# An encoder trunk of six stages on one core: x loaded from another queue, the mLSTM's divide behind its own mix, attention's sink exponentials behind the next copy of values, the last block's h ahead of a split

## The chip, the cores and the metric

The kernel runs on one core of a Trainium2 chip. A core has TensorE (PE, matrix products), VectorE (DVE), ScalarE (ACT), GpSimd (POOL) and SyncE (SP, which here only starts transfers), and 16 DMA engines that all queues share. The metric is the time of one execution on the device in microseconds (us); lower is better. The kernel before took 940.04 us, the median of three runs (939.75, 940.04, 940.04).

## The reference

The input x has 256 rows (tokens) of 1024 float32 values. Two layers follow one another, each of three steps, and every step ends in a layer norm of a scaled x plus the step's result:

```python
def swiglu(x, w_in, w_out):
    gu = x @ w_in
    g, u = gu[..., :D_FF], gu[..., D_FF:]
    return (jax.nn.silu(g) * u) @ w_out

for l in range(DEPTH):      # DEPTH = 2, D_FF = 2816
    x = layer_norm(ALPHA * x + 0.5 * swiglu(x, ffn_w_in[l, 0], ffn_w_out[l, 0]), ln_g[l, 0], ln_b[l, 0])
    y = mlstm_mixer(x, ...) if l == 0 else window_attention(x, ...)
    x = layer_norm(ALPHA * x + y, ln_g[l, 1], ln_b[l, 1])
    x = layer_norm(ALPHA * x + 0.5 * swiglu(x, ffn_w_in[l, 1], ffn_w_out[l, 1]), ln_g[l, 2], ln_b[l, 2])
```

The mLSTM mixer (layer 0) has four heads. For each head and direction the weighted scores are multiplied with the values and divided by a denominator, the two directions are added, each head is normalised and multiplied by the sigmoid of an output gate:

```python
num = einsum('bhcjs,bhcsv->bhcjv', s_qk, v) + s_inter[..., None] * einsum('bhcvd,bhcjd->bhcjv', C0, q)
den = jnp.maximum(jnp.abs(den), jnp.exp(-m_out))
h = num / den[..., None]
...
h = (h - mu) * lax.rsqrt(var + LN_EPS)
out = jax.nn.sigmoid(o) * h * norm_g
return out @ w_out
```

The attention (layer 1) has 16 query heads of 64 on four key heads, a window of 128 tokens, a distance bias, and for each head a sink: a logit that takes part in the maximum and in the sum of the softmax but has no value:

```python
m = jnp.maximum(jnp.max(s, axis=-1, keepdims=True), sink_l)
pe = jnp.exp(s - m)
attn = pe / (jnp.sum(pe, axis=-1, keepdims=True) + jnp.exp(sink_l - m))
```

## The kernel before

**Products.** Every float32 product is made of three matmuls on operands that are split in two parts: high by high, high by low, low by high. A piece of weights of 128 partitions by 1024 columns (512 KB) lands as `w_raw` or `s_raw`; ACT copies its high part (`w_hi`), DVE subtracts it from the raw piece (`w_lo`). There are ten buffers for split pieces (`RING`), four for `w_raw` and six for `s_raw`. The class `Weights` (L142 to L312) orders loads and splits; `W.done` (L294) frees used pieces and lets further ones be split. x is kept transposed as `xT_hi` and `xT_lo`: PE transposes it in pieces of 128 by 128, ACT copies the high part, DVE makes the rest. Most compute instructions are issued by one helper, so their line in the profile is L133; tiles tell them apart.

**Six stages.** FFN of layer 0 (block 0), mLSTM, FFN (block 2), FFN of layer 1 (block 3), attention, FFN (block 5). The instruction order on each engine is the order of the program. `Paced` (L49) keeps estimated times of PE, DVE, ACT and the loads, and in the FFN stages it is asked after each matmul whether a split or a sum of weights should be put in at this place; outside the FFN stages the places and numbers of splits stand in constants.

**Loads.** SP issues nearly all loads, x's four quarters among them: a quarter of x, a weight, a quarter, a weight, two quarters, then weights (L436 to L442). POOL issues the loads that add to what is in memory (L262: in each FFN group two pieces of `s_raw`) and, right at the start, seven small loads (L453 to L462): the norm's gain `gcol`, the gates' weights `gw`, the gates' four biases and the sinks.

**FFN block.** A first part of the hidden columns is computed plainly (`b_mm`, with `b_silu` on ACT and `b_mul` on DVE, whose result is `hh`). Then come three groups, in each a plain part and `seven` (L720): a form of the product that needs seven instead of eight products of half the size, on sums of x (`S1` to `S4`, made by `x_one`, `x_two`, `x_rest`) and sums of weights. Its intermediate results are called g, e and u; `tr` transposes such a piece for the second product, and its copies are called `h_hi` and `h_lo`. At a block's end `tail` computes the rest of the second product and the layer norm, whose two halves of x (x0 and x1, 128 tokens each) are transposed for the next stage; the transposes of x1 are handed over as `pending` and run inside the next stage, behind as many pieces as `PEND` says. In block 0, PE begins with 10 transposes of an identity matrix, four transposes of x, 10 more of the identity, and four more of x (L585 to L590); the results of the transposes of the identity are used nowhere.

**mLSTM.** In turns of one head: a piece of the output gate's product, `scores(h)`, `mix(h-1)` (PE makes numerators and denominators in four banks `py`; ACT takes the absolute denominators), `divide(h-2)` ahead of `scores(h)`, and `combine` and `settle` (mean and variance by DVE, the power −0.5 by POOL at L1005, which gives `hrs`, and the normalising by DVE). `divide` is a maximum and a reciprocal on `den` by DVE, two copies scaled by 1/den from PE's banks by ACT, and two multiply-adds by DVE. With the copies PE's banks come free.

**Attention.** Eleven steps (L1290). In step st, PE makes the values of head pair st−3, the transposes (`turn`) of pair st−2 in two halves, and the scores of pair st; ACT makes the four exps of the scores and two exps of the sink (`es`); POOL adds them, takes the power −1 and scales the scores in four instructions (`scale`, L1228 to L1232), which the next step's `turn` transposes. Between these lies filling work: `q_rest`, the rest of the projection of q (copied out to `q_hi` and `q_lo`), cut in steps by `QC`, and from step 4 on parts of the output projection; `FB` says how many pieces of it come ahead of the turn, `PU` how many splits of weights go in. `values` ends in a copy `q_hi` by ACT and a remainder `q_lo` by DVE.

Of the kernel before, what the change touches and what calls it, by code (L numbers as in the profile page):

```python
# [11 lines left out]
AF = mybir.ActivationFunctionType  # L12
# [16 lines left out]
PU = [2, 1, 2, 1, 1, 1, 1, 1, 0, 1, 1, 2]  # L29
QC = [4, 16, 21, 27, 32]  # L30
SW = 1
FB = [1, 0, 2, 3, 0, 0, 0, 0, 1, 1, 0]
CT = [0, 1]
LC = [1, 0, 0, 0, 0, 1]
TD = [0, 3, 2, 0, 2, 2]
MP = [1, 0, 0, 0, 1, 0, 1, 1, 0, 0, 0, 0, 2, 2, 2]
PD = [8, 0, 5, 9, 6]
PEND = [6, 4, 6, 6, 6]
# [10 lines left out]
class Paced:  # L49
# [266 lines left out]
def trunk_kernel(ctx: ExitStack, tc: tile.TileContext, x, ffn_w_in, ffn_w_out, ln_g, ln_b, ml_w_in, ml_gate_b,  # L316
# [136 lines left out]
    nc.gpsimd.dma_start(gcol, ml_norm_g[0].rearrange("(c p) -> p c", p=128))  # L453
    gw = consts.tile([128, 8, 16], F32, name="gw")
    nc.gpsimd.dma_start(gw, ml_w_in[0, :, 3072:3088].rearrange("(k p) g -> p k g", p=128))
    gbias = consts.tile([128, 1], F32, name="gbias")
    nc.gpsimd.memset(gbias, 0.0)
    for g in range(4):
        r = 64 * (g % 2) + 32 * (g // 2)
        nc.gpsimd.dma_start(gbias[r:r + 4], ml_gate_b[0, 4 * g:4 * g + 4].rearrange("(p o) -> p o", o=1))  # L460
    sink = consts.tile([128, 16], F32, name="sink")
    nc.gpsimd.dma_start(sink, bass.AP(tensor=at_sink.tensor, offset=at_sink.offset, ap=[[0, 128], [1, 16]]))  # L462
    neg_sink = consts.tile([128, 16], F32, name="neg_sink")
    nc.gpsimd.tensor_scalar(neg_sink, sink, -1.0, None, op0=OP.mult)
    neg_id = consts.tile([128, 128], FR, name="neg_id")
    nc.vector.tensor_scalar(neg_id, ident, -1.0, None, op0=OP.mult)
# [104 lines left out]
    def ffn(l, i, n, pending, last):  # L571
        with ExitStack() as ph:
# [11 lines left out]
            if start:  # L584
                warm(10)  # L585
                to_xT(0, xt[0], ybank, (0,))
                W.split(1)
                warm(10)
                to_xT(1, xt[1], ybank, (0,))
                W.split(2)  # L590
# [79 lines left out]
            else:  # L670
                W.open(pool, ends[bound[0]])
                for t in range(2):
                    ps = [wbank(), wbank()]
                    for m in range(2):
                        for a in range(4):
# [5 lines left out]
                            if t == 1 and a % 2:  # L681
                                [[None, lambda: x_raw(0), None, lambda: x_raw(1)], [None, x_one, None, x_two]][m][a]()
# [4 lines left out]
                    b_mul(sg, ps[1])  # L687
                W.done()
# [31 lines left out]
            def seven(full, unit_turn):  # L720
# [54 lines left out]
            for g in range(GROUPS):  # L775
# [34 lines left out]
                turn = seven(g < GROUPS - 1, unit_turn)  # L810
            nc.filler = None
# [7 lines left out]
    def mlstm(l, n, pending, last):  # L819
        with ExitStack() as ph:  # L820
# [227 lines left out]
            divide(2)  # L1048
# [35 lines left out]
    def attn(l, n, pending, last):  # L1084
        with ExitStack() as ph:
# [106 lines left out]
            def scores(j, between):  # L1192
# [24 lines left out]
                for t in range(2):  # L1217
# [4 lines left out]
                for a in range(2):  # L1222
                    nc.scalar.activation(es[:, :, a], nm[:, :, a], AF.Exp, bias=sink[:, 2 * j + a:2 * j + a + 1])
                stat[j] = sm, es
# [65 lines left out]
            for st in range(11):  # L1290
# [8 lines left out]
                if 0 <= st - 1 < 8:  # L1299
                    scale(st - 1)  # L1300
# [14 lines left out]
                if st < 8:  # L1315
                    scores(st, late)
# [53 lines left out]
```

## Time and profile before

| what | us |
|---|---|
| median of three runs | 940.04 |
| the profiled execution | 940.39 |
| its span, first to last instruction | 938.7 |
| PE busy | 923.0 (98%) |
| DVE busy | 795.3 (85%) |
| ACT busy | 542.9 (58%) |
| POOL busy | 103.0 (11%) |

The profile is of one execution. A row of a timeline has the start in us, the duration in us, the engine, the line, the operation, the tile written and those read, the sizes, the count, and in brackets the idle time of the engine just ahead with what ended it. A row of waits has the engine, the tile it was about to write, what it waited for, and then the total in us, the number of waits and the longest. A row of windows has the stretch in us, its length, busy time and count for PE, PEld (the load of weights into PE), DVE, ACT and POOL, then PE's granted clock as a share of the full one, the busy share of the DMA engines and the GB/s moved. Matmuls are pipelined, and busy times on PE overlap: starts tell more than durations.

### The profile page before, as it was taken

To read this page: it belongs to the slowest core of one execution; us is meant where nothing else is said; L and a number is where in the kernel's file an instruction comes from. 1 tells how busy PE (TensorE), PEld (TensorE's weight loads), DVE (VectorE), ACT (ScalarE), POOL (GpSimd) and SP (SyncE) were. 2 spreads that over 40 slices of the span, in tenths; PEclk is the share of its full clock that TensorE was granted. 3 is DMA by queue.
4 is the path that set the end of the run, shared out by engine and by line. 5 is a ranking of instruction groups with operands and counts; after the bars stand their busy time and mean duration, and the time that the engine had idled before them with its cause. 6 is when DMAs were issued, how large, how long until landed. Compare 5 with 4: busy or idle time off the path is not lost.

```text
span 938.7 us, 12456 instructions
## 1 busy us (share of the span) xinstructions
PE 923.0 (98%) x4464; PEld 768.6 (82%) x4464; DVE 795.3 (85%) x967; ACT 542.9 (58%) x765; POOL 103.0 (11%) x181
## 2 busy tenths in 40 slices
PE   8999999999999999999999999999999999999996
PEld 7888888889978788888888888887888888888885
DVE  5899997796687889988888898978877798898975
ACT  5666756347563547575635576563567554757460
POOL 2010101011110000101010101010445300000100
PEclk9999999999999999999999999999999999999998
DMA  8969773646534949695559597736533376869531
GB/s 261 367 167 331 211 258 70 221 135 197 186 97 147 316 160 314 175 340 135 163 156 347 116 329 211 270 71 221 162 132 112 90 230 241 237 212 314 159 88 45
DMA packets 98461, 187.54 MB, mean 200 GB/s; under 512 B 6720, under 2 KB 37456, under 8 KB 98400
## 3 DMA queue, kind: packets, MB, share of 16 engines
q1 hardware_dynamic: 91648, 174.09, 54.2%
q0 software_dynamic: 6752, 12.66, 8.5%
q8 instruction: 35, 0.57, 0.3%
q14 instruction: 26, 0.21, 0.1%
HBM read 185.68 MB, written 1.05 MB: 199 GB/s over the span
## 4 chain that ended last, share of the span: by engine, by line
PE 76%; DVE 11%; ACT 4%; DMA 4%; issue 3%; POOL 1%; SPq 0%; DVEq 0%; ACTq 0%; POOLq 0%
PE pw L133 47%; PE py L133 28%; DVE w_lo L133 5%; DMA w_raw<-in_ffn_w_in_dram 2%; ACT w_hi L133 2%; DMA w_raw<-in_ffn_w_out_dram 1%; DVE s_raw L133 1%; DMA s_raw<-in_ffn_w_in_dram 1%; ACT sc L133 1%; DVE x L133 1%; DVE h L133 1%; ACT S_hi L133 0%; DVE S L133 0%; DVE e L133 0%; DVE sc L133 0%
## 5 line engine op out<-in xcount | busy, mean ns | idle before, releaser
L133 DVE TENSOR_TENSOR w_lo<-w_raw,w_hi 128x1024 fp32r<-128x1024 f32 (+1 forms) x237 | 280.9, 1216 | 19.7 <-ACT w_hi L133 17.7
L133 ACT CAST w_hi<-w_raw 128x1024 fp32r<-128x1024 f32 (+1 forms) x237 | 241.1, 1048 | 78.3 <-DMA w_raw<-in_ffn_w_out_dram 22.6
L133 PE MATMUL pw<-w_hi,xT_hi 128*128 128x512 f32 x560 | 222.4, 397 | 0.2 <-ACT xT_hi L133 0.2
L133 PE MATMUL pw<-w_hi,xT_lo 128*128 128x512 f32 x560 | 218.7, 391 | 0.0
L133 PE MATMUL pw<-w_lo,xT_hi 128*128 128x512 f32 x560 | 218.3, 390 | 0.1
L133 ACT CAST w_hi<-s_raw 128x1024 fp32r<-128x1024 f32 x144 | 148.4, 1052 | 93.8 <-DVE s_raw L133 57.8
L133 DVE TENSOR_TENSOR w_lo<-s_raw,w_hi 128x1024 fp32r<-128x1024 f32 x144 | 172.6, 1219 | 21.4 <-ACT w_hi L133 21.3
L133 PE MATMUL py<-w_hi,h_hi 128*128 128x512 f32 x352 | 138.2, 393 | 0.3 <-ACT h_hi L133 0.3
L133 PE MATMUL py<-w_hi,h_lo 128*128 128x512 f32 x352 | 137.3, 390 | 0.2 <-DVE h_lo L133 0.2
L133 PE MATMUL py<-w_lo,h_hi 128*128 128x512 f32 x352 | 137.2, 390 | 0.2 <-DVE w_lo L133 0.2
L133 PEld LDWEIGHTS pw<-w_hi,xT_lo 128*128 128x128 f32 x560 | 105.1, 188 | 23.1 <-DVE xT_lo L133 0.8
L133 PEld LDWEIGHTS pw<-w_lo,xT_hi 128*128 128x128 f32 x560 | 105.3, 188 | 21.2 <-DVE w_lo L133 0.7
L133 PEld LDWEIGHTS pw<-w_hi,xT_hi 128*128 128x128 f32 x560 | 105.2, 188 | 20.6 <-ACT xT_hi L133 0.6
L133 DVE TENSOR_TENSOR s_raw<-s_raw 128x1024 f32<-128x1024 f32 x72 | 87.0, 1219 | 0.7
L262 POOL DMA_DIRECT2D s_raw<-in_ffn_w_in_dram x24 | 29.0, 1209 | 497.1 <-DVE w_lo L133 379.0
L133 PEld LDWEIGHTS py<-w_hi,h_lo 128*128 128x128 f32 x352 | 66.0, 188 | 15.1 <-DVE h_lo L133 1.4
L133 PEld LDWEIGHTS py<-w_lo,h_hi 128*128 128x128 f32 x352 | 66.1, 188 | 13.9 <-DVE w_lo L133 0.6
L133 PEld LDWEIGHTS py<-w_hi,h_hi 128*128 128x128 f32 x352 | 66.1, 188 | 13.9 <-ACT h_hi L133 0.7
L133 PE MATMUL pw<-w_hi,S_hi 128*128 128x512 f32 x192 | 74.9, 390 | 0.0
L133 PE MATMUL pw<-w_hi,S_lo 128*128 128x512 f32 x192 | 74.7, 389 | 0.0
L133 PE MATMUL pw<-w_lo,S_hi 128*128 128x512 f32 x192 | 74.7, 389 | 0.0
L133 DVE TENSOR_TENSOR h_lo<-pw,h_hi 128x512 fp32r<-128x512 f32 x44 | 30.2, 687 | 23.7 <-ACT h_hi L133 23.3
(215 smaller groups left out, 1110.0 us busy)
## 6 DMA issues: line engine op xcount, KB each, us to landing
w_raw<-in_ffn_w_out_dram SPq DMA_DIRECT2D x88, 512.0 KB, 5.3
s_raw<-in_ffn_w_in_dram SPq DMA_DIRECT2D x72, 512.0 KB, 6.1
w_raw<-in_ffn_w_in_dram SPq DMA_DIRECT2D x56, 512.0 KB, 5.3
w_raw<-in_ffn_w_in_dram SPq DMA_DIRECT2D x96, 256.0 KB, 4.5
s_raw<-in_ffn_w_in_dram POOLq DMA_DIRECT2D x24, 512.0 KB, 5.9
w_raw<-in_ml_w_in_dram SPq DMA_DIRECT2D x24, 512.0 KB, 4.6
w_raw<-in_at_w_in_dram SPq DMA_DIRECT2D x12, 512.0 KB, 4.3
w_raw<-in_ml_w_out_dram SPq DMA_DIRECT2D x8, 512.0 KB, 3.7
```

The costliest lines, as they stand in the source:

```text
L133: r = f(out, *args, **kw)
L262: nc.gpsimd.dma_start(t.rearrange("p (k f) -> p k f", k=self.words[w]["k"]), v, accum_op=OP.add)
```

## The change

- The four loads of x are issued on ACT's queue, at its very beginning, and no longer by SP; SP's queue begins with the weights.
- The seven small loads of POOL, with the clearing of the biases' tile, the negated sinks (POOL) and the negated identity `neg_id` (DVE), go into a function that is called in block 0 when its first group has been issued. They come behind the first two accumulating loads on POOL's queue.
- The transposes of the identity at the start are 14 and 8 instead of 10 and 10.
- mLSTM: `divide(h)` follows `mix(h)` at once, ahead of `settle(h-1)`; before, it came one turn later, ahead of the next scores. In the order of PE nothing moves by this.
- Attention: a pair's two sink exps, and the exps of the scores of as many halves as `EX` leaves (2 − EX[j]), go into a function `rest` that runs in the next step, behind the copy `q_hi` of values and ahead of `scale`. The first unit list `QC` gives one piece more of q's projection ahead of the first step; `FB` and `PU` are new.
- FFN blocks behind the first: `x_two` comes behind `b_mul` of the second half. In the last group of each, the transposes of u0 (and so the copy `h_hi`) come ahead of the splits of `W.done`.
- `PEND[1]` is 2 instead of 4: in block 2 the transposes of x1 come six matmuls earlier. The other changes in `PEND`, `PD` and `TD` change the number of splits at places outside the FFN blocks.

```diff
-PU = [2, 1, 2, 1, 1, 1, 1, 1, 0, 1, 1, 2]
-QC = [4, 16, 21, 27, 32]
+PU = [2, 0, 1, 2, 1, 2, 1, 1, 0, 1, 1, 4]
+QC = [5, 13, 21, 27, 32]
-FB = [1, 0, 2, 3, 0, 0, 0, 0, 1, 1, 0]
+FB = [1, 0, 1, 3, 2, 1, 0, 0, 1, 1, 0]
+EX = [0, 1, 2, 2, 2, 2, 1, 2]
-TD = [0, 3, 2, 0, 2, 2]
+TD = [0, 3, 2, 0, 2, 1]
-PD = [8, 0, 5, 9, 6]
-PEND = [6, 4, 6, 6, 6]
+PD = [8, 0, 7, 8, 5]
+PEND = [6, 2, 6, 6, 6]
...
-    def load(self, ap, source):
-        if isinstance(source, list):
+    def load(self, ap, source, engine=None):
+        if engine is not None:
+            engine.dma_start(ap, source)
+        elif isinstance(source, list):
...
-        nc.load(xt[t][:, s_], x[0, t * 128:(t + 1) * 128, s_])
+        nc.load(xt[t][:, s_], x[0, t * 128:(t + 1) * 128, s_], nc.nc.scalar)
...
+    def small_loads():
+        nc.gpsimd.dma_start(gcol, ml_norm_g[0].rearrange("(c p) -> p c", p=128))
+        nc.gpsimd.dma_start(gw, ml_w_in[0, :, 3072:3088].rearrange("(k p) g -> p k g", p=128))
+        nc.gpsimd.memset(gbias, 0.0)
+        for g in range(4):
+            r = 64 * (g % 2) + 32 * (g // 2)
+            nc.gpsimd.dma_start(gbias[r:r + 4], ml_gate_b[0, 4 * g:4 * g + 4].rearrange("(p o) -> p o", o=1))
+        nc.gpsimd.dma_start(sink, bass.AP(tensor=at_sink.tensor, offset=at_sink.offset, ap=[[0, 128], [1, 16]]))
+        nc.gpsimd.tensor_scalar(neg_sink, sink, -1.0, None, op0=OP.mult)
+        nc.vector.tensor_scalar(neg_id, ident, -1.0, None, op0=OP.mult)
...
-                warm(10)
+                warm(14)
                 to_xT(0, xt[0], ybank, (0,))
                 W.split(1)
-                warm(10)
+                warm(8)
...
-                                [[None, lambda: x_raw(0), None, lambda: x_raw(1)], [None, x_one, None, x_two]][m][a]()
+                                [[None, lambda: x_raw(0), None, lambda: x_raw(1)], [None, x_one, None, lambda: None]][m][a]()
...
                     b_mul(sg, ps[1])
+                x_two()
                 W.done()
...
-                product(qa, of(4, 1), False, end4)
+                product(qa, of(4, 1), False, end4 if full else lambda: (end4(), tr(hB, 0, v["u0"])))
                 if full:
                     down(1)
-                else:
-                    tr(hB, 0, v["u0"])
...
                 turn = seven(g < GROUPS - 1, unit_turn)
+                if start and g == 0:
+                    small_loads()
...
                 if h > 1:
-                    divide(h - 2)
                     spare()
                 scores(h, (lambda: combine(h - 2)) if h > 1 else None)
                 if h:
                     mix(h - 1)
+                    divide(h - 1)
...
-            divide(2)
             combine(2)
...
+                def exps(t):
                     s_ = sc[j, t]
                     for a in range(2):
                         nc.scalar.activation(s_[:, a], s_[:, a], AF.Exp, bias=nm[:, t, a:a + 1],
                                              scale=slope[2 * j + a], accum_out=sm[:, t, a:a + 1])
+
+                def rest():
+                    for t in range(EX[j], 2):
+                        exps(t)
+                    for a in range(2):
+                        nc.scalar.activation(es[:, :, a], nm[:, :, a], AF.Exp, bias=sink[:, 2 * j + a:2 * j + a + 1])
+                    stat[j] = sm, es
+
+                for t in range(EX[j]):
+                    exps(t)
+                return rest
...
                 if 0 <= st - 1 < 8:
+                    rest()
                     scale(st - 1)
...
-                    scores(st, late)
+                    rest = scores(st, late)
```

More of the change, by code (lines that the diff above doesn't have):

```diff
@@ L452, in trunk_kernel @@
     gcol = consts.tile([128, 8], F32, name="gcol")
-    nc.gpsimd.dma_start(gcol, ml_norm_g[0].rearrange("(c p) -> p c", p=128))
     gw = consts.tile([128, 8, 16], F32, name="gw")
-    nc.gpsimd.dma_start(gw, ml_w_in[0, :, 3072:3088].rearrange("(k p) g -> p k g", p=128))
     gbias = consts.tile([128, 1], F32, name="gbias")
[L457 to L460, printed above, removed]
     sink = consts.tile([128, 16], F32, name="sink")
-    nc.gpsimd.dma_start(sink, bass.AP(tensor=at_sink.tensor, offset=at_sink.offset, ap=[[0, 128], [1, 16]]))
     neg_sink = consts.tile([128, 16], F32, name="neg_sink")
-    nc.gpsimd.tensor_scalar(neg_sink, sink, -1.0, None, op0=OP.mult)
     neg_id = consts.tile([128, 128], FR, name="neg_id")
-    nc.vector.tensor_scalar(neg_id, ident, -1.0, None, op0=OP.mult)
+    def small_loads():
[8 more added lines that the diff above has]
+        nc.vector.tensor_scalar(neg_id, ident, -1.0, None, op0=OP.mult)
     def mm3(o, l, r, start, stop, onto=False):
@@ L1216, in scores @@
                     between()
-                for t in range(2):
+                def exps(t):
                     s_ = sc[j, t]
@@ L1221, in scores @@
                                              scale=slope[2 * j + a], accum_out=sm[:, t, a:a + 1])
-                for a in range(2):
-                    nc.scalar.activation(es[:, :, a], nm[:, :, a], AF.Exp, bias=sink[:, 2 * j + a:2 * j + a + 1])
-                stat[j] = sm, es
+                def rest():
[7 more added lines that the diff above has]
+                return rest
             def scale(j):
```

## The prediction

> **What bounds the kernel now.** I read the page first (busy shares, then the chain that ended last):
>
> ```profile
> span 938.7 us, 12456 instructions
> ...
> PE 923.0 (98%) x4464; PEld 768.6 (82%) x4464; DVE 795.3 (85%) x967; ACT 542.9 (58%) x765; POOL 103.0 (11%) x181
> ...
> PE 76%; DVE 11%; ACT 4%; DMA 4%; issue 3%; POOL 1%; SPq 0%; DVEq 0%; ACTq 0%; POOLq 0%
> ```
>
> TensorE (PE) is busy 98% and carries 76% of the chain. The change leaves the products alone, so it can only shorten the times in which PE waits. Second view, the list of PE's waits (total us, count, longest):
>
> ```profile
> PE py L133 <- DMA x<-in_x_dram: 1.5, 1, 1.5
> PE py L133 <- DVE ident L133: 1.5, 1, 1.5
> PE py L133 <- ACT h L133: 1.3, 2, 0.8
> PE pw L133 <- DVE q_lo L133: 1.0, 2, 0.8
> PE py L133 <- DVE w_lo L133: 0.4, 2, 0.2
> PE pw L133 <- DVE e L133: 0.4, 1, 0.4
> PE pw L133 <- DVE pr_lo L133: 0.3, 1, 0.3
> PE py L133 <- ACT h_hi L133: 0.3, 1, 0.3
> PE pw L133 <- DVE kp_lo L133: 0.3, 1, 0.3
> PE pw L133 <- ACT kp_hi L133: 0.2, 1, 0.2
> PE py L133 <- DVE h_lo L133: 0.2, 1, 0.2
> PE pw L133 <- ACT xT_hi L133: 0.2, 1, 0.2
> PE pw L133 <- DVE hh L133: 0.2, 1, 0.2
> ```
>
> The list holds 7.8 us in all, under 1% of the span: that is nearly all there is to win. What a wait really costs is read from the starts of the matmuls around one of them, in PE's timeline:
>
> ```profile
> 63.16 0.39 PE L133 MATMUL pw<-w_hi,S_lo 128*128 128x512 f32 x1
> 63.39 0.39 PE L133 MATMUL py<-w_hi,h_hi 128*128 128x512 f32 x1
> 63.97 0.50 PE L133 MATMUL py<-w_lo,h_hi 128*128 128x512 f32 x1 [0.20 <-DVE w_lo L133]
> 64.31 0.39 PE L133 MATMUL py<-w_hi,h_lo 128*128 128x512 f32 x1
> ```
>
> Undisturbed starts lie 0.23 apart; 63.39 to 64.31 is 0.92 for two, 0.46 too long, though the idle shown is 0.20. So a wait costs its idle plus about 0.25: the overlap of matmuls is lost too. I use that below.
>
> **Start: x by ScalarE's queue, the small loads off POOL, 14 + 8 warm-up transposes for 10 + 10.**
>
> ```profile
> 1.45 2.40 PE L133 MATMUL py<-ident 128*128 128x128 f32 x10 [1.45 <-DVE ident L133]
> ...
> 9.42 0.39 PE L133 MATMUL pw<-w_hi,xT_lo 128*128 128x512 f32 x1
> 11.27 1.26 PE L133 MATMUL py<-ident,x 128*128 128x128 f32 x8 [1.47 <-DMA x<-in_x_dram]
> 12.29 0.47 PE L133 MATMUL pw<-w_hi,xT_hi 128*128 128x512 f32 x1
> 12.77 0.50 PE L133 MATMUL pw<-w_lo,xT_hi 128*128 128x512 f32 x1
> ```
> ```profile
> 0.00:5.40 5.40, 3.95 (x18) 3.56 (x19) 0.46 (x2) 1.69 (x2) 4.10 (x12) 1.00 0.60 188
> 5.40:12.70 7.30, 5.75 (x33) 4.29 (x32) 3.79 (x6) 3.65 (x7) 2.24 (x4) 1.00 1.00 328
> ```
>
> PE finishes the first weight at 9.65 (9.42 plus one distance), then stands until x's second half has landed, at 11.27. In the windows the last two columns are the DMA engines' busy share and GB/s: 1.00 and 328 after 5.4 us, so bytes set the pace, and the order of requests decides who waits. SP's queue now sends two halves of x and two weights alternately, and x's second half third. On ACT's queue all of x leaves beside the first weights. x and two weights are 2 MB: 188 GB/s to 5.4 us gives 1.0 MB, the other 1.0 at 328 takes 3.2, so all of it is there at about 8.7 us, against 11.27 for x now. The price: x's first half shares the engines with the first weight and lands later than now, when its transposes follow the first ten at once at 3.85 (1.45 + 2.40); sharing alike with the first weight, I take 0.8 more, 4.65. The four more transposes cover it (0.24 each, so 14 end at 4.8), and the two extra in total cost under 0.5. The first weight's product so ends about 0.6 later, at 10.25; x's eight transposes follow without a wait (now 1.02, from 11.27 to 12.29, part of it the restart; I take 0.85), end 11.1, and the second weight's cast and remainder are early enough:
>
> ```profile
> 10.41 1.05 ACT L133 CAST w_hi<-w_raw 128x1024 fp32r<-128x1024 f32 x1 [2.74 <-DMA w_raw<-in_ffn_w_in_dram]
> ```
> ```profile
> 11.49 1.22 DVE L133 TENSOR_TENSOR w_lo<-w_raw,w_hi 128x1024 fp32r<-128x1024 f32 x1 [3.10 <-ACT w_hi L133]
> ```
>
> The cast waits for the landing at 10.4 and DVE for the cast, until 12.71; with all landed at 8.7 the pair ends near 11.2. So 12.29 becomes 11.1 (1.2), and the 0.25 to 0.5 lost at 12.77 goes too: 1.5. I give 0.3 back for the third weight's remainder, which then comes due sooner. **−1.2**; from −2.1 (the whole wait, 1.47 + 0.25, and the one at 12.77) to +0.3 (x no earlier, first product later).
>
> POOL's small loads also leave the first 14 us:
>
> ```profile
> q0 software_dynamic: 224, 0.08, 7.0%
> ...
> gcol<-in_ml_norm_g_dram POOLq DMA_DIRECT2D x1, 4.0 KB, 6.9
> ```
>
> 7.0% of 14 us is 1.0 us of every engine, and supports the −1.2; I count nothing more for it. The trace speaks against the gain, too: at a share of 1.00 another issuer adds no bytes, which is rival 1. The Trainium skill ("DMA: Bandwidth & Descriptors", section "Issuing engines are not separate DMA queues") says the same as a rule: transfers started by several engines interleave on the same 16 DMA engines, and issuing from several saves only the sequencer's time. The share of 1.00 agrees with the first half; whether the order in which requests arrive is worth something beside it, no run here has shown.
>
> **Small loads in their new place.** They are queued behind POOL's two accumulating loads of block 0, so at about 63.2:
>
> ```profile
> 61.96 1.21 POOL L262 DMA_DIRECT2D s_raw<-in_ffn_w_in_dram  x1 [2.24 <-DVE w_lo L133]
> ```
>
> Queued behind them on POOL are only the next group's accumulating loads; their first readers are in the mLSTM. DVE's negated identity (0.23) joins them at about 81 us. I count **0**: between 66 and 180 us the list of PE's waits is empty. The upper bound is a rival.
>
> **mLSTM: the divide behind its own mix.** In DVE's order the two settling instructions (now waiting for POOL) come behind the divide, which now starts at 257.6 behind them:
>
> ```profile
> 256.90 0.74 DVE L133 TENSOR_SCALAR h<-h,hmv,hrs 128x256 f32<-128x256 f32 x2 [0.60 <-POOL hrs L1005]
> ```
>
> The divide starts about 1.3 earlier (0.60 of waiting, 0.74 of work), so ACT's copies of h release PE's banks earlier and both waits for h go (1.3 idle, two restarts: 1.8). But DVE's work stays the same; only its 0.60 waits go, about 0.9 in two rounds once what refills them is taken off, and a later wait for w_lo (281.67, 0.2 idle) comes due sooner. So I keep half: **−0.9**, between −1.8 and −0.3.
>
> **Block 2 (second FFN): transposes of x six matmuls earlier.**
>
> ```profile
> 306.96 1.28 DVE L133 SCALAR_TENSOR_TENSOR x<-x,rs,ln_b 128x1024 f32<-128x1024 f32 x1
> 308.56 1.03 PE L133 MATMUL py<-ident,x 128*128 128x128 f32 x8
> ```
>
> Six distances are 1.4, so PE would arrive at 307.2 while x ends at 308.24: a new wait of 1.1. It frees the 0.2 (0.45) for xT_hi later, and the 0.4 (0.65) for e, since DVE works ahead where it stood. 1.1 − 0.45 − 0.65 = 0; for DVE's work kept busy I take **−0.2**, from −0.5 to +0.8 (only part comes back).
>
> **Ends of the FFN blocks.** h's copy ahead of a split: the one wait for h_hi (0.3) goes, but h_lo on DVE stays behind its e, so **−0.2** (−0.4 to 0). S2 behind the product hh: the 0.2 for hh goes, **−0.35** (−0.45 to 0). The other constants move no instruction.
>
> **Attention.** At the turn of one head's second half:
>
> ```profile
> 709.51 0.47 ACT L133 ACTIVATE es<-nm,sink 128x2 f32<-128x2 f32 x2
> ...
> 710.24 0.35 ACT L133 CAST q_hi<-pw 128x256 fp32r<-128x256 f32 x1
> ...
> 710.77 0.41 DVE L133 TENSOR_TENSOR q_lo<-pw,q_hi 128x256 fp32r<-128x256 f32 x1
> ...
> 711.24 0.66 PE L133 MATMUL pw<-ident,sc 128*128 128x128 f32 x4 [0.84 <-DVE q_lo L133]
> 711.46 1.85 POOL L1232 TENSOR_SCALAR sc<-sc,sm 128x256 f32<-128x256 f32 x4
> ```
>
> q_hi stands behind the sink exps es; with these in the next step, q_lo comes 0.4 sooner, and the work dealt ahead of the turn covers the rest. The list shows five waits in this stage: 1.8 idle, 3.0 with restarts. The one at 711.24 goes (1.1), those at the start shrink with the added q matmuls (0.6), one more of 0.3 to 0.5 goes: 2.1. Given back: 0.6, where two splits now come ahead of q_lo on DVE in one step. **−1.5**; from −2.2 to +0.7. The sink exps themselves (0.47 for two) stay on ACT, which is 58% busy; who waits for them is POOL's scaling (1.85 for four), read by the next turn.
>
> **Sum.** −1.2 − 0.9 − 0.2 − 0.2 − 0.35 − 1.5 = −4.35. The profiled execution took 940.39, its span 938.7 and 1.7 outside, and stands 0.35 above the median of 940.04. 940.39 − 4.35 = **936.0**.
>
> **The rivals.** (1) x comes no earlier: engines at 1.00 carry the same bytes, and only issues are saved. For it: that share; against: x's second half is third in the queue now. Without the −1.2 it is 937.3 (rounded up). (2) The sink exps make POOL late: they now follow another copy on ACT, POOL's chain for a head starts after them, and turns wait for POOL instead of q_lo. Against: the chain for a head has until the next step. −1.5 becomes +0.7: 938.2. Both together: 939.5. (3) Slower: the small loads at 63.2 hold the weight stream. For it: alone at the start gcol took 6.9 from issue to landing for 4 KB and the row at 63.97 shows the lead of w_lo there at nothing, so a hold of 6.9 could reach PE whole: 936.0 + 6.9 = 942.9. It decides from a hold of 4.4 on. Against it: by the 7.0% above all the small loads together took 1.0 of each engine, a seventh of that hold, and between 66 and 180 PE waits for nothing; a hold of 1.0 would give 937.0.
>
> **How the numbers follow.** Forecast 0.61, (1) 0.14, (2) 0.10, both 0.07, (3) 0.08. The forecast's own range is 934.0 to 938.2: about half of the terms' bounds, since they won't all fall on one side. To hold 8 in 10 it goes from 933.8 to 939.6, which takes in (1), (2) and both. A measurement tells 0.2% (1.9 us) from no change: faster is below 938.2, slower above 941.9. Faster: nearly all of the forecast, most of (1), half of (2): 0.75. Slower: (3) and mishaps not listed: 0.10. Same: 0.15.
>
> **What would show it.** Right: no wait for x, second weight near 11 us; no waits for h; in attention none above 0.5 for q_lo; a new wait of about 1 us at 307. Wrong: x's transposes still wait past 11; waits for w_lo between 64 and 80; turns waiting for POOL's sc.

## The result and the profile after

The changed kernel takes 935.21 us (median of 5 runs, 934.8 to 936.01) against 940.04 for the kernel before (5 runs, 938.35 to 940.48). The ratio is 0.9953 with a 95% interval of 0.994 to 0.9966: 0.5% faster. The forecast was 936.0 with a range of 933.8 to 939.6. The profiled execution took 935.12.

Its page has these lines (busy shares, then the chain that ended last); the span is 933.4:

```profile
PE 920.0 (99%) x4466; PEld 769.0 (82%) x4466; DVE 795.5 (85%) x967; ACT 541.4 (58%) x765; POOL 101.5 (11%) x181
...
PE 83%; DVE 9%; DMA 2%; ACT 2%; issue 2%; SPq 1%; POOL 0%; DVEq 0%; ACTq 0%; POOLq 0%
```

No engine has much less to do (PE is busy 920.0 us for 923.0). PE carries 83% of the chain for 76% before, which fits that fewer of its waits are left. The list of PE's waits in the changed kernel (total us, count, longest; the helper's line is now L136):

```profile
PE py L136 <- DVE ident L136: 1.5, 1, 1.5
PE py L136 <- DVE x L136: 0.9, 1, 0.9
PE pw L136 <- ACT e L136: 0.9, 1, 0.9
PE py L136 <- DMA x<-in_x_dram: 0.7, 2, 0.4
PE pw L136 <- DVE h L136: 0.5, 1, 0.5
PE py L136 <- DVE h_lo L136: 0.4, 2, 0.2
PE pw L136 <- DVE kp_lo L136: 0.3, 1, 0.3
PE py L136 <- DVE w_lo L136: 0.2, 1, 0.2
PE pw L136 <- DVE w_lo L136: 0.2, 1, 0.2
PE pw L136 <- DVE pr_lo L136: 0.2, 1, 0.2
```

The waits for x's transfer (1.5 before), for ACT's h (1.3) and for q_lo (1.0) are gone or small. The largest new ones are 0.9 for DVE's x and 0.9 for ACT's e, both in block 2; a new 0.5 for DVE's h lies in the mLSTM. Following the same matmul through both traces tells where the 5.3 us of the span went. The first two columns are its start in PE's timeline; the third is the change over the stage, the difference between one row's shift and the next's.

| up to | before | after | stage's change | forecast |
|---|---|---|---|---|
| first group of block 0 | 64.31 | 62.74 | −1.57 | −1.2 |
| gates of the mLSTM | 200.74 | 199.11 | −0.06 | 0 |
| end of the mLSTM | 282.00 | 279.01 | −1.36 | −0.9 |
| block 2 | 464.98 | 462.98 | +0.99 | −0.2 |
| end of block 3 | 644.53 | 641.94 | −0.59 | −0.2 |
| attention's first scores | 687.52 | 684.92 | −0.01 | 0 |
| attention's last values | 740.07 | 735.24 | −2.23 | −1.5 |
| end of the span | 938.7 | 933.4 | −0.47 | −0.35 |

(The row for block 2 reaches to the first products of block 3.) Five rows have the forecast sign and are larger; one, block 2, has the other sign. Each column is one execution. The same rows in the traces of the experiments below, where these leave a stage as it is in the changed kernel, show how far one trace goes: the first row lies between −1.21 and −2.35, the mLSTM between −1.07 and −1.39, block 2 between +0.31 and +1.30, attention between −2.21 and −2.27. Where a stage is said to stand at a figure below, it is this change against the kernel before, in the trace of the run in question.

### The profile page after: what moved, and what is told of

The parts are those of the page before. It is cut to its first block, busy times and chain, and to the rows that moved or that the text cites. A ratio compares the mean times of both kernels' runs of the same rounds, so it can differ in the third digit from the quotient of the medians.

```text
span 933.4 us, 12457 instructions
## 1 busy us (share of the span) xinstructions
PE 920.0 (99%) x4466; PEld 769.0 (82%) x4466; DVE 795.5 (85%) x967; ACT 541.4 (58%) x765; POOL 101.5 (11%) x181
## 3 DMA queue, kind: packets, MB, share of 16 engines
q10 hardware_dynamic: 576, 1.05, 0.3%
HBM read 185.68 MB, written 1.05 MB: 200 GB/s over the span
## 4 chain that ended last, share of the span: by engine, by line
PE 83%; DVE 9%; DMA 2%; ACT 2%; issue 2%; SPq 1%; POOL 0%; DVEq 0%; ACTq 0%; POOLq 0%
PE pw L136 54%; PE py L136 29%; DVE w_lo L136 4%; DMA w_raw<-in_ffn_w_in_dram 1%; ACT w_hi L136 1%; DMA s_raw<-in_ffn_w_in_dram 1%; DVE x L136 1%; DVE h L136 1%; DVE s_raw L136 0%; DVE wt L136 0%; DVE h_lo L136 0%; SPq L102 0%; DVE a_lo L136 0%; ACT h L136 0%; DVE hst L136 0%
## 5 line engine op out<-in xcount | busy, mean ns | idle before, releaser
L136 DVE TENSOR_TENSOR w_lo<-w_raw,w_hi 128x1024 fp32r<-128x1024 f32 (+1 forms) x237 | 281.4, 1219 | 19.1 <-ACT w_hi L136 16.9
L136 ACT CAST w_hi<-w_raw 128x1024 fp32r<-128x1024 f32 (+1 forms) x237 | 240.9, 1049 | 73.2 <-DMA w_raw<-in_ffn_w_in_dram 19.2
L136 PE MATMUL pw<-w_hi,xT_hi 128*128 128x512 f32 x560 | 222.2, 397 | 0.0
L136 PE MATMUL pw<-w_hi,xT_lo 128*128 128x512 f32 x560 | 218.7, 390 | 0.0
L136 PE MATMUL pw<-w_lo,xT_hi 128*128 128x512 f32 x560 | 218.3, 390 | 0.2 <-DVE w_lo L136 0.2
L136 ACT CAST w_hi<-s_raw 128x1024 fp32r<-128x1024 f32 x144 | 148.4, 1052 | 97.7 <-DVE s_raw L136 62.0
L136 DVE TENSOR_TENSOR w_lo<-s_raw,w_hi 128x1024 fp32r<-128x1024 f32 x144 | 172.9, 1220 | 21.5 <-ACT w_hi L136 21.4
L136 PE MATMUL py<-w_hi,h_hi 128*128 128x512 f32 x352 | 138.0, 392 | 0.0
L136 PE MATMUL py<-w_hi,h_lo 128*128 128x512 f32 x352 | 137.3, 390 | 0.4 <-DVE h_lo L136 0.4
L136 PE MATMUL py<-w_lo,h_hi 128*128 128x512 f32 x352 | 137.1, 390 | 0.0
L136 PEld LDWEIGHTS pw<-w_hi,xT_lo 128*128 128x128 f32 x560 | 105.1, 188 | 22.6 <-DVE xT_lo L136 0.2
L136 PEld LDWEIGHTS pw<-w_lo,xT_hi 128*128 128x128 f32 x560 | 105.3, 188 | 21.2 <-DVE w_lo L136 0.7
L136 PEld LDWEIGHTS pw<-w_hi,xT_hi 128*128 128x128 f32 x560 | 105.2, 188 | 20.0
L136 DVE TENSOR_TENSOR s_raw<-s_raw 128x1024 f32<-128x1024 f32 x72 | 87.1, 1220 | 0.6
L136 PEld LDWEIGHTS py<-w_hi,h_lo 128*128 128x128 f32 x352 | 66.1, 188 | 15.3 <-DVE h_lo L136 1.6
L136 PEld LDWEIGHTS py<-w_lo,h_hi 128*128 128x128 f32 x352 | 66.1, 188 | 13.8 <-DVE w_lo L136 0.3
L136 PEld LDWEIGHTS py<-w_hi,h_hi 128*128 128x128 f32 x352 | 66.1, 188 | 13.2
L136 PE MATMUL pw<-w_hi,S_hi 128*128 128x512 f32 x192 | 74.8, 390 | 0.9 <-ACT e L136 0.9
L136 PE MATMUL pw<-w_hi,S_lo 128*128 128x512 f32 x192 | 74.7, 389 | 0.0
L136 PE MATMUL pw<-w_lo,S_hi 128*128 128x512 f32 x192 | 74.7, 389 | 0.0
L136 DVE TENSOR_TENSOR h_lo<-pw,h_hi 128x512 fp32r<-128x512 f32 x44 | 30.2, 688 | 23.9 <-ACT h_hi L136 23.7
```

The lines of the kernel that those rows point to most:

```text
L136: r = f(out, *args, **kw)
```

## The experiments

All are the changed kernel with one thing altered. Runs of one kernel scatter by 0.5 to 4 us (one by 6), so times tell apart about 1 us; what is smaller is read from the traces, where a wait has a place. The table puts the ratios side by side.

| altered | median us | ratio to the kernel before, 95% interval |
|---|---|---|
| nothing (the changed kernel) | 935.21 | 0.9953 [0.994, 0.9966] |
| PEND[1] back at 4 | 935.02 | 0.9948 [0.9936, 0.996] |
| x by SP | 935.72 | 0.996 [0.9947, 0.9972] |
| x by SP, 10 and 10 transposes | 935.63 | 0.9954 [0.9941, 0.9966] |
| small loads early | 936.56 | 0.9968 [0.9957, 0.9979] |
| divide at its old places | 937.11 | 0.9972 [0.9962, 0.9983] |
| attention as before | 938.33 | 0.9987 [0.9976, 0.9997] |
| all exps in place, new lists | 937.37 | 0.9976 [0.9967, 0.9985] |
| old lists, exps late | 940.94 | 1.0011 [0.9999, 1.0024] |
| x_two and u0's transposes as before | 935.79 | 0.9957 [0.9943, 0.9971] |
| one sum less in block 2 | 934.95 | 0.9948 [0.9934, 0.9962] |
| S3 and S4 by POOL | 936.11 | 0.9963 [0.9951, 0.9976] |
| e ahead of two casts in block 2 | 936.2 | 0.9956 [0.9943, 0.997] |

### The start: which of its three edits

x issued by SP again:

```diff
-        nc.load(xt[t][:, s_], x[0, t * 128:(t + 1) * 128, s_], nc.nc.scalar)
+        nc.load(xt[t][:, s_], x[0, t * 128:(t + 1) * 128, s_])
```

> The changed kernel with x issued by SP again, in the order of before; small loads late and 14 and 8 transposes as changed. Theory (the order of requests counts): x's second half is third in the queue again, PE's transposes of it start later than 11 instead of at 10.3, and the first 64 us lose 1 us or more: about 936.4. Rival (the same bytes, only issues saved; what helped were the small loads' absence): x lands as now within 0.3, and the time stays at 935.2 to 935.5.

PE's timeline of this run, around x's second half:

```profile
10.39 1.03 PE L136 MATMUL py<-ident,x 128*128 128x128 f32 x8
11.18 0.48 PE L136 MATMUL pw<-w_hi,xT_hi 128*128 128x512 f32 x1
```

and of the changed kernel:

```profile
10.30 1.04 PE L136 MATMUL py<-ident,x 128*128 128x128 f32 x8
11.10 0.47 PE L136 MATMUL pw<-w_hi,xT_hi 128*128 128x512 f32 x1
11.79 0.50 PE L136 MATMUL pw<-w_lo,xT_hi 128*128 128x512 f32 x1 [0.22 <-DVE w_lo L136]
```

With x back on SP, its second half in its old third place, the eight transposes still start at 10.39 without a wait, and the second weight at 11.18 for 11.10. The median, 935.72, is 0.2 above the rival's range and within the scatter. So the queue is not what moved x. The theory falls, the rival holds.

The small loads at the start again, x staying on ACT's queue:

```diff
-                if start and g == 0:
-                    small_loads()
...
         nc.vector.tensor_scalar(neg_id, ident, -1.0, None, op0=OP.mult)
+
+    small_loads()
```

> The changed kernel with the seven small loads, the negated sinks and the negated identity at the start again; x on ACT's queue. Theory: the small loads cost the start at most what their share of the engines says, 0.5 to 1.0: 935.4 to 936.2, GB/s from 5.4 to 12.7 us back from 361 towards 328. Rival one (the hold moves to block 0): with them gone from 63 us nothing changes there, since nothing was lost there. Rival two: they hold back weights for several us at the start; then PE waits over 1.5 more in the first 40 us, 936.7 or more.

PE's timeline there:

```profile
10.21 0.60 PE L136 MATMUL py<-ident,x 128*128 128x128 f32 x4
12.46 0.63 PE L136 MATMUL py<-ident,x 128*128 128x128 f32 x4 [1.65 <-DMA x<-in_x_dram]
12.84 0.48 PE L136 MATMUL pw<-w_hi,xT_hi 128*128 128x512 f32 x1
```

The wait for x is back, 1.65, although x is issued first on a queue of its own. With the kernel before (SP, small loads early, a wait of 1.47) all four combinations of queue and small loads are measured: the wait goes with the small loads. The windows from 5.4 to 12.7 us (the last column is GB/s) of the changed kernel, of x by SP, and of the small loads early:

```profile
5.40:12.70 7.30, 6.70 (x40) 5.34 (x39) 4.78 (x7) 5.02 (x8) 0.00 (x0) 1.00 0.97 361
```
```profile
5.40:12.70 7.30, 6.44 (x39) 5.38 (x38) 4.86 (x7) 4.93 (x8) 0.00 (x0) 1.00 1.01 360
```
```profile
5.40:12.70 7.30, 5.65 (x31) 4.95 (x30) 4.41 (x6) 3.84 (x6) 1.21 (x4) 1.00 1.05 321
```

Without the small loads the same engines, as busy, move 361 or 360 GB/s; with them 321 (328 in the kernel before). The rival of a hold of several us is the nearer one: the run is 1.4 slower by the medians (936.56, just short of that rival's 936.7), 2.0 by the spans of the two traces. Which of the seven loads does it was not tried.

The third of the edits, with x by SP too:

```diff
-                warm(14)
+                warm(10)
...
-                warm(8)
+                warm(10)
```

> The changed kernel with x issued by SP in the order of before and 10 and 10 transposes, so that of the start's three edits only the late small loads are left. Theory, from the run in which only the queue was undone: the small loads alone bring the start's gain, and the time is that of the changed kernel within 0.5, 934.7 to 935.7. Rival: the 14 transposes are what the later arrival of x's first quarter needs only on ACT's queue, and with 10 PE starts its first weight 0.5 to 0.9 earlier: 934.3 to 934.7.

935.63 and a ratio of 0.9954: nothing is lost, and by the first row of the table above this trace stands at −1.66, for −1.57 in the changed kernel and −0.11 with the small loads early. Of the start's three edits, the late small loads alone bring the gain.

### The mLSTM

```diff
+                    divide(h - 2)
                     spare()
...
                     mix(h - 1)
-                    divide(h - 1)
...
+            divide(2)
             combine(2)
```

> The changed kernel with the mLSTM's divide back at its old places; all else as changed. Theory: the two waits for h return (1.3 idle, 1.8 with restarts) and the wait for h at 271 (0.5) goes: 1.2 to 1.5 slower, 936.4 to 936.7. Rival: DVE's chain sets the end of this stage, and the waits return without costing more than 0.5: 935.7.

The waits of PE between 240 and 290 us in this run:

```profile
PE py L136 <- ACT h L136: 1.3, 2, 0.8
PE py L136 <- DVE w_lo L136: 0.2, 1, 0.2
```

They are the two of the kernel before to the tenth, and the 0.5 for DVE's h goes. The theory holds; the medians say 1.9, the traces 1.4 in this stage.

### Attention

Lists and exps as before together:

```diff
-PU = [2, 0, 1, 2, 1, 2, 1, 1, 0, 1, 1, 4]
-QC = [5, 13, 21, 27, 32]
-FB = [1, 0, 1, 3, 2, 1, 0, 0, 1, 1, 0]
+PU = [2, 1, 2, 1, 1, 1, 1, 1, 0, 1, 1, 2]
+QC = [4, 16, 21, 27, 32]
+FB = [1, 0, 2, 3, 0, 0, 0, 0, 1, 1, 0]
...
-                for t in range(EX[j]):
-                    exps(t)
-                return rest
+                for t in range(2):
+                    exps(t)
+                for a in range(2):
+                    nc.scalar.activation(es[:, :, a], nm[:, :, a], AF.Exp, bias=sink[:, 2 * j + a:2 * j + a + 1])
+                stat[j] = sm, es
...
-                    rest()
                     scale(st - 1)
```

> The changed kernel with the attention stage's lists (PU, QC, FB) and the places of its exps as before; all else as changed. Theory: the stage loses the 2.2 again that the traces show between the start of the scores and the last values: about 937.4, with the wait of 0.8 for q_lo back. Rival: the stage's gain comes from what is ahead of it (PE 2.6 us earlier), and only 1 us or less returns: 936.2 or less.

938.33, 3.1 above the changed kernel, and the waits for q_lo are back (1.0 in two). In this trace attention stands at +0.01 against the kernel before, so its whole 2.23 is gone: the theory holds. The rest of the 3.1 is not attention's; this trace loses 1.1 in block 0, mainly at a wait of 0.8 for e near 121, where nothing was altered.

The exps alone in place again, with the new lists:

> The changed kernel with all exps, those of the sinks too, in the step of their scores again; the new lists PU, QC and FB stay. Theory: the sink exps stand ahead of q_hi on ACT again, about 0.4 in each of six steps, of which one to two steps show it as a wait: 0.5 to 1.2 slower, 935.7 to 936.4. Rival: the lists alone bring the gain, 935.2 within 0.3.

PE's waits between 678 and 745 us:

```profile
PE pw L136 <- DVE pr_lo L136: 0.6, 1, 0.6
PE pw L136 <- DVE q_lo L136: 0.3, 1, 0.3
```

937.37, 2.2 slower, more than expected: not only q_lo but also pr_lo, which follows ACT's pr_hi, is late when the sink exps stand where they stood. Attention stands at −0.60 against the kernel before, so the new lists alone bring 0.6 of the 2.23.

The lists alone as before, the exps late:

> The changed kernel with the old lists PU, QC and FB and the exps at their new places. Theory: filling work is missing ahead of the first scores and the turns again, 1.0 to 1.7 slower: 936.2 to 936.9. Rival: the places of the exps alone bring the gain, 935.2 within 0.3.

940.94: 5.7 slower, and no better than the kernel before. Neither expectation reached so far. Attention stands at +2.84 against the kernel before. PE's timeline, then POOL's, and then windows of this run (us, busy of PE, PEld, DVE, ACT, POOL, PE's granted clock, DMA share, GB/s):

```profile
694.30 0.28 PE L136 MATMUL py<-xT_hi,w_lo 128*128 128x256 f32 x1
696.14 1.85 PE L136 MATMUL pw<-ident,sc 128*128 128x128 f32 x4 [1.55 <-POOL sc L1246]
698.21 0.63 PE L136 MATMUL pw<-kp_lo,q_hi 128*128 128x512 f32 x1
698.64 0.63 PE L136 MATMUL pw<-kp_hi,q_lo 128*128 128x512 f32 x1
```
```profile
693.62 0.20 POOL L1242 TENSOR_TENSOR sm<-sm,es 128x4 f32<-128x4 f32 x1 [11.35 <-ACT es L136]
693.89 1.03 POOL L1243 TENSOR_TENSOR sm<-sm,minus_one 128x4 f32<-128x4 f32 x1
695.02 2.43 POOL L1246 TENSOR_SCALAR sc<-sc,sm 128x256 f32<-128x256 f32 x4
```
```profile
694.00:697.60 3.60, 1.78 (x9) 0.93 (x9) 1.22 (x1) 2.83 (x11) 3.50 (x6) 0.90 0.23 64
697.60:700.30 2.70, 2.70 (x7) 2.07 (x8) 0.99 (x5) 2.28 (x3) 2.52 (x6) 0.51 1.03 414
700.30:704.00 3.70, 3.70 (x33) 3.68 (x32) 3.67 (x9) 2.88 (x11) 0.38 (x1) 1.00 0.19 70
```

This is the prediction's second rival, seen in full. POOL starts its chain on the sum behind the late exps (693.62) and scales from 695.02; the turn's four transposes wait 1.55 for the first part and then go at POOL's pace, one per part. In the window behind that PE's granted clock is 0.51 for 2.7 us: matmuls start 0.43 apart for 0.23. In the changed kernel POOL is earlier:

```profile
691.43 1.85 POOL L1246 TENSOR_SCALAR sc<-sc,sm 128x256 f32<-128x256 f32 x4
```

The new lists put 8 pieces of q's projection into the first step instead of 12, so ACT reaches the late exps at 687.50 instead of 691.10, POOL has scaled by 693.28, and the turn starts at 693.35 without a wait. Against the kernel before, the new lists alone bring 0.6, the late exps alone cost 2.8, and the two together bring 2.2: the late exps are worth something only with the new lists.

### The ends of the FFN blocks

```diff
-                                ... [None, x_one, None, lambda: None]][m][a]()
+                                ... [None, x_one, None, x_two]][m][a]()
...
-                x_two()
...
-                product(qa, of(4, 1), False, end4 if full else lambda: (end4(), tr(hB, 0, v["u0"])))
+                product(qa, of(4, 1), False, end4)
                 if full:
                     down(1)
+                else:
+                    tr(hB, 0, v["u0"])
```

> The changed kernel with x_two at its old place and the last group's transposes of u0 behind the splits again. Theory: the waits for h_hi at the end of block 3 (0.56 against 0.28 left) and for hh in block 5 (0.4) return: 0.6 to 1.0 slower, 935.8 to 936.2. Rival: what stands behind takes them up, 935.2 within 0.3.

935.79, 0.6 slower by the medians and within the scatter. The wait for h_hi (0.3) is back at 641, and this trace stands at −0.20 in block 3 for −0.59. The wait for hh in block 5 is not back, so the rest of the change suffices to remove it. In the run with attention as before, where S2 has its new place, it is absent too. So either is enough; that it is attention's lists in the first case, and not `PD` or `TD`, was not tried apart.

### Block 2: where 1 us was lost

Four runs are about this stage. PE's two new waits in the changed kernel:

```profile
305.31 1.09 PE L136 MATMUL py<-ident,x 128*128 128x128 f32 x8 [0.94 <-DVE x L136]
```
```profile
356.31 0.50 PE L136 MATMUL pw<-w_hi,S_hi 128*128 128x512 f32 x1 [0.86 <-ACT e L136]
```

The first run puts PEND[1] back:

```diff
-PEND = [6, 2, 6, 6, 6]
+PEND = [6, 4, 6, 6, 6]
```

> The changed kernel with PEND[1] back at 4, all else as changed. In the changed kernel PE waits 0.9 for x at 305 and 0.9 for e at 356 in block 2, 2.2 lost with restarts; the kernel before lost 1.3 there at other places (312, 366). Theory: the six matmuls' earlier transposes are the cause of both (the first directly, the second through one remainder of weights more that the planner puts ahead of the sums on DVE), so both new waits go and the two old ones return: 1.0 faster than the changed kernel, about 934.2. Rival: DVE's work is the limit in block 2 once PE is 3 us ahead there, and the wait only moves: 935.2, with the loss of 2.2 found at other places of block 2.

Waits of PE between 296 and 375 us, PEND[1] at 4:

```profile
PE pw L136 <- DVE e L136: 0.8, 1, 0.8
PE pw L136 <- ACT xT_hi L136: 0.4, 1, 0.4
```

Both new waits go; the old ones return larger (0.8 for 0.4 and 0.4 for 0.2 in the kernel before). Block 2 stands at +0.93 for +0.99, and the time is 935.02, that of the changed kernel. The rival holds: the loss moves. The run with x_two at its old place shows a third distribution (same window):

```profile
PE pw L136 <- DVE hh L136: 1.0, 1, 1.0
PE py L136 <- DVE x L136: 0.9, 1, 0.9
```

What is late at 356? ACT's timeline in the changed kernel, then ACT's and PE's in the kernel before at the same place:

```profile
353.78 2.00 ACT L136 CAST w_hi<-s_raw 128x1024 fp32r<-128x1024 f32 x2 [3.15 <-DVE s_raw L136]
355.68 0.58 ACT L136 COPY e<-pw 128x512 f32<-128x512 f32 x1
```
```profile
354.57 2.19 ACT L133 CAST w_hi<-s_raw 128x1024 fp32r<-128x1024 f32 x2 [1.36 <-DVE s_raw L133]
356.66 0.58 ACT L133 COPY e<-pw 128x512 f32<-128x512 f32 x1
```
```profile
357.86 0.39 PE L133 MATMUL pw<-w_hi,S_hi 128*128 128x512 f32 x1
```

The copy of e, which gives PE its bank back, stands behind two casts of weights, and the first of these waits 3.15 for a sum on DVE. In the kernel before it stood behind two such casts as well, but that cost nothing: PE came to this place at 357.86. Now PE would be there 2.6 us earlier (at 355.29, one distance behind its matmul at 355.06), while the casts start only 0.8 earlier. So two theories: DVE has too much to do, or the place in ACT's queue. One sum less on DVE (the sum is left out; the planner still counts its time, so that the order stays):

```diff
-            nc.vector.tensor_add(t, t, self.raw[v])
+            if self.nth == 22:
+                nc.on_vector("tensor_add", D, [t], [t, self.raw[v]])
+            else:
+                nc.vector.tensor_add(t, t, self.raw[v])
+            self.nth += 1
```

> The changed kernel without one sum of weights on DVE in block 2 (128x1024, 1.22 us, the one between h_lo and e at 347); the sum is left out, so the products that use it differ. Theory: in block 2 DVE's work ahead of the copy e sets when PE goes on at 356, so 1.1 less work there takes most of the 1.1 lost at 356: 0.7 to 1.1 faster than the changed kernel, 934.1 to 934.5, if nothing behind it gives it back. Rival: the landing of weights or ACT's own work sets it, and the wait at 356 stays above 0.8.

934.95, and the wait is 0.7 for 0.9, neither the theory's size nor quite the rival's 0.8. It looks as if PE saw only 0.2 of the 1.2 us taken away. DVE's rows say more; the changed kernel first, then this run:

```profile
344.44 0.68 DVE L136 TENSOR_TENSOR S<-xr,xr 128x512 f32<-128x512 f32 x1
...
352.53 1.22 DVE L136 TENSOR_TENSOR s_raw<-s_raw 128x1024 f32<-128x1024 f32 x1
```
```profile
345.09 0.69 DVE L136 TENSOR_TENSOR S<-xr,xr 128x512 f32<-128x512 f32 x1
...
352.04 1.22 DVE L136 TENSOR_TENSOR s_raw<-s_raw 128x1024 f32<-128x1024 f32 x1
```

From the sum of x to the sum of weights that ACT waits for, DVE takes 8.09 in the changed kernel and 6.95 here: 1.14 less, nearly the whole sum. But it came into this stretch 0.65 later, ahead of the place of the edit: a cast of ACT at 323.83 waits 1.58 for a landing, for 0.33 in the changed kernel. And PE came 0.3 earlier. So e is copied only 0.49 earlier (355.19 for 355.68). Without the late landing it would have been about 1.1, and the wait would be gone; this is an estimate from these rows. In the eight traces in which block 2 is that of the changed kernel the wait here lies between 0.18 and 1.18. The run does not settle it, and its rows speak for the theory: with this order on ACT, DVE's work sets when e is copied. Then two sums of x taken from DVE to POOL:

```diff
-                nc.vector.tensor_tensor(f, a, b, op=op)
+                if name in ("S4", "S3"):
+                    nc.gpsimd.tensor_tensor(f, a, b, op=op)
+                    nc.mark(f, max(nc.vec, nc.pe) + 1500.0)
+                else:
+                    nc.vector.tensor_tensor(f, a, b, op=op)
```

> The changed kernel with the sums S4 and S3 of x made by POOL instead of DVE in all four FFN blocks (two of 0.69 us each less on DVE in each block). Theory (DVE's work is what block 2 waits for): the wait at 356 shrinks by most of 1.1, other blocks hide it anyway: 934.0 to 934.7. Rival: ACT's copies and DVE's remainders of S4 and S3 now wait for POOL, which is slower than DVE, and the casts behind them come late: 935.2 to 937.

The wait at 356 is gone, but the order on ACT is another too (e's copy comes ahead of the casts here), PE comes there 2 us later (357.25), and block 0 pays: between 20 and 200 us PE waits 1.6 for w_lo in three waits, where the changed kernel has none. The time is 936.11. Block 2 gains, but this run can't tell the two theories apart. Last, the order alone:

```diff
-            if act < nc.pe + AHEAD and ...
+            if not self.hold and act < nc.pe + AHEAD and ...
...
+                W.hold = bound[0] == 2 and g == 0
                 product(qa, sum_("S2"), False, end6)
...
                     v["u0"] = copied(qa, "e2")
+                    W.hold = False
```

> The changed kernel with one order altered in block 2's first group: ACT's copy of e (with the Silu behind it) stands ahead of the two casts of weights that wait for DVE's sum, not behind them; a few casts and remainders behind it change places by this. DVE's sums stay where they are. Theory: the 1.1 lost at 356 is this place in ACT's queue and nothing else; e is copied near 353 and PE goes on at 355.3: 0.8 to 1.1 faster than the changed kernel, 934.1 to 934.5, and a version better than both. Rival: PE then meets the same lateness at the remainder of weights or at the next e some us later (as in the run with PEND[1] at 4, 1.0 at 365), and the time stays at 935.0 to 935.4.

ACT's timeline in this run:

```profile
352.11 0.59 ACT L136 COPY e<-pw 128x512 f32<-128x512 f32 x1 [2.13 <-PE pw L136]
...
353.15 2.95 ACT L136 CAST w_hi<-s_raw 128x1024 fp32r<-128x1024 f32 x3
```

e is copied at 352.11, the casts start as before (353.15 for 353.78, in a trace that is 0.7 ahead at x's transposes), and of PE's waits between 296 and 375 us only the 0.9 for x is left. Block 2 stands at −0.16 for +0.99, and the profiled execution has the shortest span of all, 932.6. In that trace, with DVE's sum as late against PE as in the changed kernel, another place in ACT's queue alone removes the 1.1 at 356, and it comes back nowhere in block 2; a wait for e of 0.5 appears at 804, in block 5, where nothing was altered. But the times don't confirm a gain: five runs from 934.3 to 937.35, median 936.2. Whether this version is faster than the changed kernel stays open.

## Why the prediction was right, and where it was not

**Time, sign and range** were right: 935.2 for 936.0. The reading that PE's 98% leaves only its waits to win held: PE's products are the same and the gain lies where waits went.

**Start (−1.2, measured −1.57): near in size, wrong in cause.** The step that failed is "the order of requests decides who waits" together with "I count nothing more for it" about the small loads. It was the reverse: undoing the queue changed nothing (10.39 for 10.30 at x's transposes), undoing the small loads' place brought a wait of 1.65 back. The share of 7.0%, or 1.0 us, was too low a measure of what these loads do to others: 361 GB/s became 321, and the run was 1.4 slower. x's transposes (10.30) and the second weight (11.10) do start where the forecast put them (10.25 and 11.1): the price for the later first product was right, but that x had landed by then is luck, since the landing at 8.7 was worked out from x's queue (5.4 and 3.2 make 8.6, besides). The second weight's wait did not go as said: 0.22 for w_lo stands at 11.79, and behind it the gain is 0.97 (12.13 for 13.10). The other 0.6 comes later, at 38 and 64 us; the run with the small loads early gains 0.4 there too, so most of it is not theirs. The first rival was half right: the queue saves nothing, but the time for it, 937.3, assumed that nothing else brings the gain. The Trainium skill ("DMA: Bandwidth & Descriptors", section "Issuing engines are not separate DMA queues") had the queue's part right; both runs with x on SP agree with it (transposes of x's second half at 10.39 and 10.48, for 10.30 with x on ACT's queue).

**Small loads at 63 us (0, measured −0.06 up to the gates): right.** They do hold others there. Landing times among the issues between 58 and 75 us, first the kernel before, then the changed one:

```profile
s_raw<-in_ffn_w_in_dram SPq DMA_DIRECT2D x6, 512.0 KB, 5.8
...
w_raw<-in_ffn_w_out_dram SPq DMA_DIRECT2D x1, 512.0 KB, 5.3
```
```profile
s_raw<-in_ffn_w_in_dram SPq DMA_DIRECT2D x6, 512.0 KB, 7.2
...
w_raw<-in_ffn_w_out_dram SPq DMA_DIRECT2D x2, 512.0 KB, 7.0
```

1.4 to 1.7 more, far from the 4.4 from which the third rival would decide, and PE felt none of it in this trace. In two of the other eleven traces with the loads there (PEND[1] at 4, attention as before) block 0 loses 0.6 and 1.1 behind 64 us, at a wait for e near 121; whether the small loads have a part in that is not shown.

**mLSTM (−0.9, measured −1.36).** The mechanism was right; the half kept back for DVE was too much. The new wait is the 0.5 for h at 271, not a larger one for w_lo.

**Block 2 (−0.2, measured +0.99, outside its own bound of +0.8).** The new wait at the transposes of x was forecast as 1.1 and came as 0.94 idle, 1.1 by starts. The step that failed is "the 0.4 (0.65) for e, since DVE works ahead where it stood": the wait at 366 went, but 0.86 idle came at 356 on another copy of e. The forecast looked at the six matmuls alone and not at PE's coming some 3 us earlier out of the stages before, which DVE's sums did not follow (casts 0.8 earlier, PE 2.6): the copy, behind two casts as before, now came too late. That PEND is not the cause is shown by the run with 4 in it (+0.93). The sum gave 0 besides; the −0.2 taken instead has no row behind it.

**Ends (−0.2 and −0.35, measured −0.59 and −0.47).** The wait for h_hi went, and one of 0.2 for h_lo stands at 641.6, as said. For hh the term was near in size, but the place of S2 was not needed for it.

**Attention (−1.5, measured −2.23).** The mechanism was right: the waits for q_lo are gone. The 0.6 said to be given back behind two splits did not appear. The rival in which POOL becomes the limit is real, as the run with the old lists shows (5.7 slower), and it was the new lists that kept it away. The forecast priced them at 0.6 for the start of the stage; alone they bring as much, but without them the late exps cost 2.8.

The closeness of the total owes something to luck: block 2 was 1.2 worse and the other terms together 2.1 better than said.

## What to carry to other kernels

Small loads that nobody needs yet should not be issued while the first large transfers are on their way: here 0.08 MB cost 1.4 us, more than their bytes or their share of busy time (1.0 us) say. When an engine gets an instruction that waits for another engine, look at what is queued behind it: in attention it was q_hi behind sink exps, in block 2 the copy of e behind casts, and moving such a copy ahead of them removed PE's wait in both (in attention with the new lists). Such a place can cost nothing until another edit brings PE there earlier. And before a small effect of an experiment is believed, look whether its trace came into the stretch as early as the other. Undo an edit's parts one at a time and in pairs: one of three parts brought the start's gain, and two parts of attention were worth 2.2 us together, while the late exps alone were worse than neither.

## What the runs showed of the hardware that was not expected

PE's clock fell to half in attention with the old lists and late exps. PE's dense work ended at 694.58; then came a pause of 1.55 and transposes at 696.14 and 696.60. In windows of half a us the granted clock is 1.00 up to 696.5, 0.86 to 697.0 and 0.50 from there to 700.0, although the matmuls are dense again from 697.6; it is back at 1.00 from 700.5. The wait of 1.65 for x with the small loads early, after which full work followed at once, left the matmuls at 0.23 and 0.32 apart and the clock at 1.00. So in these two traces not the longest pause alone decides; how little PE does over some us seems to, which no run here tests. The Trainium skill ("TensorE: Matmul & The Clock Gate", Part 1) gives idle windows of about 3.4 us for the fall; here it came 1.9 to 2.4 us after the dense work, and that stretch wasn't empty.

Transfers of POOL's queue amounting to 0.08 MB took the rate of the 16 DMA engines from 361 to 321 GB/s over 7.3 us, 0.3 MB less, while these engines' busy share was no lower (1.05 for 0.97).
